# Row maxima of a 64 MB tensor: two load blocks in place of four, and eight late rows reduced by way of TensorE and GpSimd

## The chip, the cores and the metric

The kernel runs on one core of a Trainium2 chip. The metric is the device time in microseconds (us) of one execution; ten executions of the kernel before are shown below. Besides these times there is one profiled execution, whose span runs from the first to the last instruction that the hardware profiler recorded. Engines are named as in the profile: PE is TensorE, DVE is VectorE, ACT is ScalarE, POOL is GpSimd and SP is SyncE, which here only issues the loads.

## The reference

```python
def setup_inputs():
    batch, seq, dim = 32, 512, 1024
    return {"x": np.random.randn(batch, seq, dim).astype(np.float32)}

def reference(x):
    return np.max(x, axis=-1).astype(np.float32)
```

There are 32 x 512 = 16384 rows of 1024 floats (67.11 MB in), and the result is one maximum for each row (16384 floats out). A maximum costs one comparison for each element that is read.

## The kernel before

The 16384 rows are spread over the 128 partitions, so each partition has 128 rows of 4 KB. "A row" below always means one row on each of the 128 partitions, which is 512 KB. The rows are cut into four blocks of 42, 35, 34 and 17 rows per partition; inside a block a partition owns consecutive rows of `x`, so that a load of `g` rows reads `4 * g` KB in one piece for each partition. `BLOCKS` lists the loads of each block:

```python
BLOCKS = [
    [15, 14, 13],
    [11, 9, 8, 7],
    [6, 6, 5, 4, 4, 4, 3, 2],
    [2, 2, 2, 2, 2, 1, 1, 1, 1, 1, 1, 1],
]
RING = 46
```

One loop goes over the blocks and one inside it over the loads, 27 in all. For each load, SP issues a DMA of `g` rows into the next free place of `ring` (line 51), a buffer of 46 rows per partition in SBUF; when a load doesn't fit behind the last one, the place starts at 0 again (`at = 0`). VectorE then reduces these rows along the free dimension to `g` columns of `res` (line 52). `res` holds the 128 results of each partition. Behind each block ScalarE's queue issues a store of that block's columns (line 56). TensorE is not used, and GpSimd only fills four constants at the start.

The order is set by the tile framework. It keeps each engine's instructions in a list, puts a wait before a reduce for its load, and puts a wait before a load for the reduces that still read the place it overwrites. The loads also share eight completion semaphores in turn, so that a load waits for the landing of the load eight places ahead of it. SP issues in program order, and VectorE works in program order: a reduce that waits holds up all reduces behind it.

The wrapper at the end of the file only declares the tensors and launches the program. In the profile, a line 73 or 84 stands for the launch's own work at the start and at the end.

Of the kernel before, what the change touches and what calls it, by code (L numbers as in the profile page):

```python
# [1 line left out]

# [4 lines left out]


F32 = mybir.dt.float32

BLOCKS = [
    [15, 14, 13],
    [11, 9, 8, 7],
    [6, 6, 5, 4, 4, 4, 3, 2],
    [2, 2, 2, 2, 2, 1, 1, 1, 1, 1, 1, 1],
]
RING = 46


@with_exitstack
def kernel(
    ctx: ExitStack,
    tc: tile.TileContext,
    x: bass.AP,
    out: bass.AP,
):
    nc = tc.nc
    P = 128  # L30
    X = mybir.AxisListType.X

    xf = x.flatten_outer_dims()
    N, D = xf.shape
    I = N // P
    of = out.flatten_outer_dims()

    once = ctx.enter_context(tc.tile_pool(name="once", bufs=1))
    ring = once.tile([P, RING, D], F32)
    res = once.tile([P, I], F32)  # L40

    at = first = 0
    for loads in BLOCKS:
        S = sum(loads)
        xb = xf[first * P:(first + S) * P, :].rearrange("(p i) d -> p i d", p=P)
        b = 0
        for g in loads:
            if at + g > RING:
                at = 0
            xc = ring[:, at:at + g, :]  # L50
            nc.sync.dma_start(out=xc, in_=xb[:, b:b + g, :])  # L51
            nc.vector.reduce_max(out=res[:, first + b:first + b + g], in_=xc, axis=X)  # L52
            at += g
            b += g
        dst = bass.AP(tensor=of.tensor, offset=of.offset + first * P, ap=[[S, P], [1, S]])
        nc.scalar.dma_start(out=dst, in_=res[:, first:first + S])
        first += S
    assert first == I


# [1 line left out]
_INS = ['x']  # L62
_OUTS = [((32, 512), 'float32')]


# [23 lines left out]
```

## Time and profile before

| | us |
|---|---|
| median of 10 runs | 165.67 (165.49 to 165.97) |
| the profiled execution's own time | 165.66 |
| its span | 163.9 |
| VectorE busy, 27 reduces | 138.4 |
| VectorE's first reduce starts | 21.7 |
| VectorE's last reduce ends | 161.5 |
| GpSimd busy | 0.2 |
| bytes read, mean rate over the span | 67.11 MB, 410 GB/s |

The time of the profiled execution is 1.76 us longer than its span, and its last store takes 1.4 us to land. In the lines that follow, a group of instructions reads: line, engine, operation, output `<-` input, their shapes, and a count; then the busy time in us and the mean of one in ns; then the idle time of the engine just ahead of them and what ended it. A line of a load reads: tile `<-` tensor, queue, operation and count, the size in KB, and the us from its issue to its landing. SPq and ACTq are the queues of SP and ACT, and DVEq is VectorE's sequencer.

### The profile page before, as it was taken

Reading aid. Unit: us, or ns where it says so; the run is one execution under the profiler, and the core shown is the slowest. Engines: PE = TensorE matmul, PEld = TensorE weight load, DVE = VectorE, ACT = ScalarE, POOL = GpSimd, SP = SyncE. Lnnn points to the kernel's source line nnn. Section 1 sums busy time; section 2 is a strip of 40 time slices with the busy share of each in tenths; the row PEclk is TensorE's granted clock in tenths of the full one; section 3 lists DMA queues with packets and bytes.
Section 4 is the critical chain, followed back from the end, with each engine's and each line's share of the span. In section 5 each row is a group of like instructions: output and inputs, shape, how many; then the busy total and the mean of one; then the engine's idle time right before and its main releaser. Section 6 shows DMA issues by size and latency. Waiting matters only on the chain.

```text
span 163.9 us, 114 instructions
## 1 busy us (share of the span) xinstructions
DVE 138.4 (84%) x27; POOL 0.2 (0%) x4
## 2 busy tenths in 40 slices
DVE  0000079998999899999999999999999999999994
POOL 0000000000000000000000000000000000000000
DMA  7999699999999989999999999999999999999970
GB/s 240 480 480 450 270 448 448 448 448 416 416 416 449 495 352 528 414 433 420 402 408 440 441 407 468 396 455 408 421 440 436 409 425 418 422 420 416 404 310 2
DMA packets 4464, 67.18 MB, mean 410 GB/s; under 512 B 1008, under 2 KB 1008, under 8 KB 1904
## 3 DMA queue, kind: packets, MB, share of 16 engines
q1 hardware_dynamic: 3888, 67.11, 96.1%
q10 hardware_dynamic: 576, 0.07, 0.3%
HBM read 67.11 MB, written 0.07 MB: 410 GB/s over the span
## 4 chain that ended last, share of the span: by engine, by line
DVE 74%; DMA 23%; DVEq 1%; another core or an unknown queue 0%; SPq 0%; issue 0%
DVE res L52 74%; DMA ring<-in_x_dram 23%; DVEq L84 1%; SPq L51 0%
## 5 line engine op out<-in xcount | busy, mean ns | idle before, releaser
L52 DVE TENSOR_REDUCE res<-ring 128x1 f32<-128x1024 f32 (+12 forms) x27 | 138.4, 5200 | 23.1 <-DMA ring<-in_x_dram 23.1
L73 POOL MEMSET const-bfloat16-1.0<- 128x1 bf16 x1 | 0.1, 101 | 0.0
L73 POOL MEMSET const-uint8-127<- 128x1 uint8 x1 | 0.1, 101 | 0.0
L73 POOL MEMSET const-float32-0.0<- 128x1 f32 x1 | 0.1, 98 | 0.2 <-issue 0.2
L73 POOL MEMSET const-float32-1.0<- 128x1 f32 x1 | 0.1, 98 | 0.0
## 6 DMA issues: line engine op xcount, KB each, us to landing
ring<-in_x_dram SPq DMA_DIRECT2D x1, 7680.0 KB, 20.9
ring<-in_x_dram SPq DMA_DIRECT2D x1, 7168.0 KB, 37.4
ring<-in_x_dram SPq DMA_DIRECT2D x1, 6656.0 KB, 52.7
ring<-in_x_dram SPq DMA_DIRECT2D x2, 3072.0 KB, 33.4
ring<-in_x_dram SPq DMA_DIRECT2D x3, 2048.0 KB, 33.9
ring<-in_x_dram SPq DMA_DIRECT2D x6, 1024.0 KB, 24.0
ring<-in_x_dram SPq DMA_DIRECT2D x1, 5632.0 KB, 29.8
ring<-in_x_dram SPq DMA_DIRECT2D x1, 4608.0 KB, 24.9
```

What stands on the lines that cost most here:

```text
L52: nc.vector.reduce_max(out=res[:, first + b:first + b + g], in_=xc, axis=X)
L73: nc = _bacc.Bacc("TRN2", target_bir_lowering=False, num_devices=1)
L84: with _tile.TileContext(nc) as tc:
```

## The change

There are now two blocks, of 112 and 16 rows per partition, and the ring has 45 places. Each load is a triple `(n, m, w)`: `n` rows are loaded, the last `m` of them take a second route, and `w` is the number of the load behind whose reduce the result of that route is due. The loads are 15, 14, 14, 15, 15, 13, 12, 8 and 6 rows, then 4, 2, 2 and seven single rows, and the last row comes as two halves of 512 columns, one into `ring` and one into `tail`: 21 loads.

Eight rows take the second route (three of the seventh load, one of the eighth, two of the ninth, one of the tenth and one of the twelfth). For each of them TensorE turns the row's 1024 columns in eight transposes of 128 x 128 into PSUM (`ps`), so that the 128 partitions' rows lie along the free dimension; ScalarE copies `ps` to SBUF (`sb`); GpSimd takes the maximum over the partitions with `partition_all_reduce` (`top`); and eight small transposes turn `top` back into eight columns of `back`, one for each piece of 128 columns. VectorE then reduces these eight columns to the result. `backs` and `due` place the turns back and these last reduces in the program.

The identity matrix for the transposes is made on GpSimd behind the first load. The maximum of the last row's first half is written next to the second half in `tail`, and the last reduce takes both. Both stores now stand at the end of the program; the first of them is made to wait for the reduce of the last single row.

```diff
 BLOCKS = [
-    [15, 14, 13],
-    [11, 9, 8, 7],
-    [6, 6, 5, 4, 4, 4, 3, 2],
-    [2, 2, 2, 2, 2, 1, 1, 1, 1, 1, 1, 1],
+    [(15, 0, -1), (14, 0, -1), (14, 0, -1), (15, 0, -1), (15, 0, -1), (13, 0, -1), (12, 3, 7), (8, 1, 9), (6, 2, 12)],
+    [(4, 1, 14), (2, 0, -1), (2, 1, 17), (1, 0, -1), (1, 0, -1), (1, 0, -1), (1, 0, -1), (1, 0, -1), (1, 0, -1), (1, 0, -1)],
 ]
-RING = 46
+RING = 45
...
+    turn = ctx.enter_context(tc.tile_pool(name="turn", bufs=2))
+    allr = ctx.enter_context(tc.tile_pool(name="allr", bufs=2))
+    psum = ctx.enter_context(tc.tile_pool(name="psum", bufs=3, space=bass.MemoryType.PSUM))
+    psmall = ctx.enter_context(tc.tile_pool(name="psmall", bufs=2, space=bass.MemoryType.PSUM))
...
+    ident = once.tile([P, P], F32)
+    PAD = 16
+    tail = once.tile([P, PAD + H], F32)
+    backs = []
+    due = {}
+    def by_gpsimd(rows, cols, m):
+        back = psmall.tile([P, m, C], F32)
+        for k in range(m):
+            ps = psum.tile([P, D], F32)
+            for c in range(C):
+                nc.tensor.transpose(
+                    out=ps[:, c * P:(c + 1) * P],
+                    in_=rows[:, k, c * P:(c + 1) * P],
+                    identity=ident,
+                )
+            sb = turn.tile([P, D], F32)
+            nc.scalar.copy(out=sb, in_=ps)
+            top = allr.tile([P, D], F32)
+            nc.gpsimd.partition_all_reduce(top, sb, P, bass_isa.ReduceOp.max)
+            run(backs)
+            def turn_back(top=top, k=k):
+                for c in range(C):
+                    nc.tensor.transpose(
+                        out=back[:, k, c:c + 1],
+                        in_=top[0:1, c * P:(c + 1) * P],
+                        identity=ident[0:1, 0:1],
+                    )
+            backs.append(turn_back)
+        return lambda: nc.vector.reduce_max(out=cols, in_=back, axis=X)
+    def run(calls):
+        while calls:
+            calls.pop(0)()
...
-        for g in loads:
-            if at + g > RING:
+        for n, m, w in loads:
+            if at + n > RING:
                 at = 0
-            xc = ring[:, at:at + g, :]
-            nc.sync.dma_start(out=xc, in_=xb[:, b:b + g, :])
-            nc.vector.reduce_max(out=res[:, first + b:first + b + g], in_=xc, axis=X)
...
-        nc.scalar.dma_start(out=dst, in_=res[:, first:first + S])
+            xc = ring[:, at:at + n, :]
+            nc.sync.dma_start(out=xc, in_=xb[:, b:b + n, :])
+            cols = res[:, first + b:first + b + n]
+            if m:
+                due.setdefault(w, []).append(by_gpsimd(xc[:, n - m:, :], cols[:, n - m:], m))
+            else:
+                run(backs)
+            if j == 0:
+                nc.gpsimd.tensor_copy(out=ident[:, 0:1], in_=xc[:, 0, 0:1])
+                make_identity(nc, ident)
+            if n > m:
+                reduce = nc.vector.reduce_max(out=cols[:, :n - m], in_=xc[:, :n - m, :], axis=X)
+            run(due.get(j, []))
...
+    half = ring[:, at, :H]
+    nc.sync.dma_start(out=half, in_=xb[:, b, :H])
+    nc.sync.dma_start(out=tail[:, PAD:], in_=xb[:, b, H:])
+    nc.vector.reduce_max(out=tail[:, PAD - 1:PAD], in_=half, axis=X)
+    nc.vector.reduce_max(out=res[:, I - 1:], in_=tail[:, PAD - 1:], axis=X)
+    store = nc.scalar.dma_start(out=views[0][0], in_=views[0][1])
+    tc.add_manual_dep(store.ins, reduce.ins.name, SYNC, reason="behind the loads")
+    nc.scalar.dma_start(out=views[1][0], in_=views[1][1])
```

Here `D` is 1024, `P` 128, `C = D // P` is 8 and `H = D // 2` is 512.

More of the change, by code (lines that the diff above doesn't have):

```diff
@@ L6 @@
 from concourse._compat import with_exitstack
+from concourse import bass_isa
+from concourse.masks import make_identity
 F32 = mybir.dt.float32
 BLOCKS = [
-    [15, 14, 13],
-    [11, 9, 8, 7],
-    [6, 6, 5, 4, 4, 4, 3, 2],
-    [2, 2, 2, 2, 2, 1, 1, 1, 1, 1, 1, 1],
-]
-RING = 46
+    [(15, 0, -1), (14, 0, -1), (14, 0, -1), (15, 0, -1), (15, 0, -1), (13, 0, -1), (12, 3, 7), (8, 1, 9), (6, 2, 12)],
+    [(4, 1, 14), (2, 0, -1), (2, 1, 17), (1, 0, -1), (1, 0, -1), (1, 0, -1), (1, 0, -1), (1, 0, -1), (1, 0, -1), (1, 0, -1)],
+]
+RING = 45
+SYNC = mybir.DependencyInfo(mybir.DependencyClass.Sync, mybir.DependencyReason.DATA)
 @with_exitstack
@@ L34 @@
     N, D = xf.shape
+    H = D // 2
+    C = D // P
     I = N // P
@@ L38 @@
     once = ctx.enter_context(tc.tile_pool(name="once", bufs=1))
+    turn = ctx.enter_context(tc.tile_pool(name="turn", bufs=2))
+    allr = ctx.enter_context(tc.tile_pool(name="allr", bufs=2))
+    psum = ctx.enter_context(tc.tile_pool(name="psum", bufs=3, space=bass.MemoryType.PSUM))
+    psmall = ctx.enter_context(tc.tile_pool(name="psmall", bufs=2, space=bass.MemoryType.PSUM))
     ring = once.tile([P, RING, D], F32)
     res = once.tile([P, I], F32)
-    at = first = 0
+    ident = once.tile([P, P], F32)
@@ L43 @@
+    def run(calls):
+        while calls:
+            calls.pop(0)()
+    at = first = j = 0
+    views = []
     for loads in BLOCKS:
-        S = sum(loads)
+        S = sum(n for n, m, w in loads) + (loads is BLOCKS[-1])
         xb = xf[first * P:(first + S) * P, :].rearrange("(p i) d -> p i d", p=P)
+        dst = bass.AP(tensor=of.tensor, offset=of.offset + first * P, ap=[[S, P], [1, S]])
+        views.append((dst, res[:, first:first + S]))
         b = 0
-        for g in loads:
-            if at + g > RING:
+        for n, m, w in loads:
+            if at + n > RING:
@@ L49 @@
                 at = 0
-            xc = ring[:, at:at + g, :]
-            nc.sync.dma_start(out=xc, in_=xb[:, b:b + g, :])
[L52 to L55, printed above, removed]
-        nc.scalar.dma_start(out=dst, in_=res[:, first:first + S])
+            xc = ring[:, at:at + n, :]
+            nc.sync.dma_start(out=xc, in_=xb[:, b:b + n, :])
@@ L57 @@
+            at += n
+            b += n
+            j += 1
         first += S
     assert first == I
+    half = ring[:, at, :H]
[5 more added lines that the diff above has]
+    tc.add_manual_dep(store.ins, reduce.ins.name, SYNC, reason="behind the loads")
```

## The prediction

> **What bounds the kernel now.** I read the page's busy row and slices first, then the chain that ended last, then the reduces kept apart by shape, then the loads' times to landing.
>
> ```profile
> DVE 138.4 (84%) x27; POOL 0.2 (0%) x4
> ...
> DMA  7999699999999989999999999999999999999970
> ```
>
> Two resources look full: VectorE (DVE) and the DMA engines. The chain says which one ends last:
>
> ```profile
> 1.14 37.44 DMA ring<-in_x_dram
> 38.59 0.02 issue
> 38.61 15.09 DVE res L52
> 53.70 0.62 another core or an unknown queue
> 54.32 0.02 issue
> 54.34 106.06 DVE res L52 x24
> 160.40 1.13 DVEq L84
> ```
>
> Columns are start, length and what. After 54.34 us VectorE runs without a gap until 161.53, so VectorE ends the kernel. The shapes give its price per row:
>
> ```profile
> L52 DVE TENSOR_REDUCE res<-ring 128x15 f32<-128x15360 f32 x1 | 16.2, 16152 | 21.7 <-DMA ring<-in_x_dram 21.7
> L52 DVE TENSOR_REDUCE res<-ring 128x14 f32<-128x14336 f32 x1 | 15.1, 15087 | 0.8 <-DMA ring<-in_x_dram 0.8
> ...
> L52 DVE TENSOR_REDUCE res<-ring 128x1 f32<-128x1024 f32 x7 | 8.0, 1208 | 0.0
> ```
>
> One row more costs 16152 - 15087 = 1065 ns. A single row lasts 1208 ns, but the last two start at 159.2 and 160.3, about 1.13 us apart, so queued reduces overlap a little: I count 1.067 us a row plus 0.06 an instruction. Then the loads:
>
> ```profile
> ring<-in_x_dram SPq DMA_DIRECT2D x1, 7680.0 KB, 20.9
> ring<-in_x_dram SPq DMA_DIRECT2D x1, 7168.0 KB, 37.4
> ring<-in_x_dram SPq DMA_DIRECT2D x1, 6656.0 KB, 52.7
> ```
>
> Issued near 0.7, 1.1 and 1.6 us, they land at 21.6, 38.6 and 54.3: 32.7 us for 27 rows, 1.21 us a row, slower than VectorE's 1.07. The last load (issued at 150.2, landing 9.6 us later) lands at 159.8, and late single rows come 1.2 to 1.3 us apart. The loads therefore end 1.7 us before VectorE: that is nearly all there is to win, as every byte must still come.
>
> **What the Trainium skill says.** "DMA: Bandwidth & Descriptors", Where 436 GB/s comes from, puts the ports' ceiling at 435 GB/s, which is 1.205 us for a 512 KB row; 1.21 in this trace agrees, so the new load sizes cannot speed the stream. "VectorE: DVE Perf Modes", The perf-mode tier table, gives `tensor_reduce` one element a cycle only; 1065 ns for 1024 elements agrees. "GPSIMD Engine Reference", Performance versus the Vector engine, and Cross-partition, price the new operation below; nothing here shows it.
>
> **The change part by part.** *Loads.* Row counts landed become 15, 29, 43, 58, 73, 86, 98, 106, 112, 116 and on. At 1.21 us a row with some 0.05 us for each load the first seven land at 21.6, 38.6, 55.5, 73.7, 91.8, 107.6 and 122.2. VectorE waits for the second to fifth 0.9, 1.9, 3.1 and 2.0 us, and 0.2 for the seventh: 8 us in place of 1.4, so 6.6 lost. The seventh's nine rows end at 122.2 + 9.7 = 131.9. Ring space: the fifth load needs slots freed by the third reduce, at 70.6, while the fourth is in flight until 73.7; 3 us cover its start. Later loads wait only on reduces done by 122 and on earlier loads, so a late VectorE does not stop the stream. It ends at 159.3.
>
> *Reduces.* Left after 131.9: 7, 4, 3 and 2 rows (7.53 + 4.33 + 3.26 + 2.19), eight single rows (9.02), two half rows (0.59 + 0.68), five reduces of `back`, 8 to 24 elements (I take 0.15 each from a single row's 0.14 over its elements: 0.75). That is 28.35 us: without a further wait VectorE ends at 160.25, 1.3 us sooner. The half rows cost one instruction and spare waiting for the last half; the loads' end plus one half reduce, 160.0, bounds this from below.
>
> *The new route.* Each of eight rows takes eight TensorE transposes, a ScalarE copy, a GpSimd maximum and eight small transposes; then VectorE reads `back`. The diff interleaves them, but the changed program's TensorE list, as the scheduler leaves it (T a row's turn, B its turn back), is
>
> ```
> T1 T2 T3 B1 B2 B3 | T4 B4 | T5 T6 B5 B6 | T7 B7 | T8 B8
> ```
>
> and VectorE's list has the reduce of B1 to B3 *before* the eighth load's seven rows. Every bar makes GpSimd run dry: T4 stands behind B3, which waits for GpSimd's third maximum. Each group then pays turn, copy and turn back in series.
>
> Prices: "TensorE: Matmul & The Clock Gate", PE-mode transpose, gives 275 ns for a transpose in a kernel, for bf16; eight make 2.2 us. "ScalarE: Activation LUTs", What ACT_TABLE_LOAD costs, gives 186 ns + 0.833 ns an element: 1.0 us. Eight turns back of one column I take at 1.0 (half), hops between engines at 0.2: together c = 4.4 us, from 2.5 (if consecutive transposes take 0.1 us) to 6. The maximum X over 128 partitions by 1024 columns: I count some 14 operations a column (read, write, four folds of shuffle and maximum over a core's 16 lanes, four for the neighbours); at the page's three a cycle and 1.2 GHz that is 4.0 us. The page's own best loop takes 1.8 cycles where its ports allow 1.03, and that factor gives 7.0. I take X = 5.5. Ends: 1.5 us, the price of one plain loop over 1024 columns (1.8 cycles each); and 124 us, half the page's 247.7 us for a partition-axis reduce of 2048 columns.
>
> The chain starts at 122.2:
> - B3 done at 122.2 + 4.4 + 3 x 5.5 = 143.1; VectorE, free at 131.9, stands 11.2 us.
> - B4: 143.1 + 4.4 + 5.5 = 153.0; VectorE through its seven rows at 150.8: 2.2.
> - B6: 153.0 + 4.4 + 11.0 = 168.4; its four rows done at 157.5: 10.9.
> - B7: 178.3; 3 + 2 rows done at 174.0: 4.3.
> - B8: 188.2; three singles done at 181.8: 6.4.
>
> The stalls sum to 35.0 us; VectorE ends at 160.3 + 35.0 = 195.3. Behind each waiting reduce stand all later reduces, and both stores wait for the last of them.
>
> *Hidden parts.* The identity and GpSimd's library load start after the first landing at 21.6, 100 us before use. ScalarE's table load comes before its first copy. The first store (57 KB) now starts one single and two half reduces before the end; it should land beside the last one. If not, up to 1 us more.
>
> *Sum.* The profiled execution took 165.66 us: 161.53 to VectorE's end, 2.37 to the span's end (a store of 1.4 us and closing), 1.76 around the span; the median of the runs, 165.67, is the same. 195.3 + 2.4 + 1.7 = **199.4 us**. In general: 122.2 + 5c + 8X + 7.1 + 4.1.
>
> **The rivals.** *GpSimd is quick and the waits vanish.* VectorE ends at 160.3 and the time is 164.4. B8 must be done by 154.4, so X at most 1.3 us with c = 4.4, or 2.5 with c = 2.5. For it: VectorE does lose 8.5 us of rows. Against: the price of one plain loop would have to fold 128 partitions. 6%, and 2% for an end within 0.2% of before.
>
> *GpSimd reduces as slowly as the page's reduce:* X = 124 gives 122.2 + 22 + 992 + 11.2 = 1147 us. Nothing in the trace excludes it; the page's figure is for another instruction. Anything over X = 9.5: 7%.
>
> *The change doesn't do what it says in the other sense:* were the diff's interleaving kept, GpSimd would run without gaps from 125.4, and the end would be 125.4 + 8 x 5.5 + 1.1 + 7.1 + 4.1 = 181.7. The lists speak against it; 5%.
>
> *The stream slows* because rows of one partition now lie 448 KB and 64 KB apart instead of 68 to 168. Each per cent until the seventh landing adds 1.2 us. The chain stays the end, so it only widens the range.
>
> **How the numbers follow.** The main case, X from 3 to 9.5 us with the lists as they are, has 80%. Its ends: X = 3, c = 3 gives 172.5; X = 9, c = 5 gives 230.4. The range 172 to 230 takes in the interleaved case and leaves out the quick and the very slow one. Chances: faster by over 0.2% (about what a measurement of this kernel can tell from no change) 0.06, within 0.2% 0.02, slower 0.92.
>
> **What would show it.** Right: waits of VectorE for TensorE in five places, near 11, 2, 11, 4 and 6 us; five bursts of TensorE; GpSimd's maxima some 5.5 us apart inside a burst with a gap near 4 us between bursts; the last load landing near 159; VectorE free at 131.9. The prediction is wrong in its price if consecutive maxima start under 2 or over 9.5 us apart, in its order if T4 precedes B3 in the trace, and altogether if VectorE shows no wait for TensorE and ends near 160.

## The result, and the profile after

| | before | changed |
|---|---|---|
| median, us | 165.57 (165.40 to 165.97, 29 runs) | 181.9 (181.02 to 182.39, 8 runs) |
| ratio | 1 | 1.0972 [1.0958, 1.0987] |
| profiled execution: time, span | 165.66, 163.9 | 182.32, 180.5 |
| VectorE's last reduce ends | 161.5 | 178.1 |
| the last load lands | 159.9 | 161.3 |

The change makes the kernel 16.3 us slower. The forecast was slower by 33.7: the direction and the mechanism held, and one price was far too high. The lines below, of the changed kernel, are the page's busy time of each engine and the share of the DMA engines in 40 slices of the span (9 is 90% or more); the prediction shows the same lines of before:

```profile
PE 21.6 (12%) x128; PEld 19.4 (11%) x128; DVE 130.7 (72%) x26; ACT 9.4 (5%) x9; POOL 26.6 (15%) x15
...
DMA  6999999999999999999989989999999999920000
```

VectorE has 7.7 us less to do (130.7 in place of 138.4), and still ends 16.6 us later. The DMA row is full through its 35th slice and then empty: in the last 19 us there is nothing left to load, and no engine is busy all the time. So something waits. The list of waits (engine, line, what it waited for: total us, times, longest) says what:

```profile
POOL top L74 <- ACT sb L72: 110.9, 5, 94.3
DVE res L115 <- DMA ring<-in_x_dram: 31.7, 6, 21.4
...
DVE res L86 <- PE back L79: 15.7, 4, 5.9
```

VectorE waits 15.7 us for TensorE's turns back, in four places; before, nothing of the kind existed. It also waits 31.7 us for loads, where it waited 23.1 before. That accounts for its later end: 15.7 + 8.6 - 7.7 = 16.6. GpSimd waited 94.3 us for its first row, and four times more for ScalarE's copies, together 16.6 us. The timeline of one pass from bar to bar shows how the two belong together. Its columns are start, length, engine, line and operation, and in brackets the idle time just ahead and what ended it:

```profile
127.50 9.68 POOL L74 PARTITION_ALL_REDUCE top<-sb  x3 [94.28 <-ACT sb L72]
...
137.23 1.01 PE L79 MATMUL back<-ident,top 1*128 1x1 f32 x8 [2.19 <-POOL top L74]
138.17 1.57 PEld L66 LDWEIGHTS ps<-ident,ring 128*128 128x128 f32 x8
138.18 1.97 PE L66 MATMUL ps<-ident,ring 128*128 128x128 f32 x8
138.28 0.18 DVE L86 TENSOR_REDUCE res<-back 128x3 f32<-128x24 f32 x1 [4.26 <-PE back L79]
138.38 7.61 DVE L115 TENSOR_REDUCE res<-ring 128x7 f32<-128x7168 f32 x1
140.24 1.01 ACT L72 COPY sb<-ps 128x1024 f32<-128x1024 f32 x1 [8.45 <-PE ps L66]
141.34 3.22 POOL L74 PARTITION_ALL_REDUCE top<-sb  x1 [4.16 <-ACT sb L72]
```

Three maxima end at 137.2. Only then does TensorE turn the third one back (1.01 us) and, behind that, turn the fourth row (1.97), which had been in SBUF since about 134; ScalarE copies it (1.01), and GpSimd, dry for 4.16 us, starts again. VectorE stood 4.26 us for the turn back, with seven loaded rows queued behind. The same bracket, 4.16, stands at each of the four bars (a bar is a place in TensorE's order where the turn of a row stands behind a turn back that waits for GpSimd).

### The profile page after: what moved, and what is told of

Read it like the earlier page. It is cut to its first block, busy times and chain, and to the rows that moved or that the text cites. A ratio compares the mean times of both kernels' runs of the same rounds, so it can differ in the third digit from the quotient of the medians.

```text
span 180.5 us, 400 instructions
## 1 busy us (share of the span) xinstructions
PE 21.6 (12%) x128; PEld 19.4 (11%) x128; DVE 130.7 (72%) x26; ACT 9.4 (5%) x9; POOL 26.6 (15%) x15
## 4 chain that ended last, share of the span: by engine, by line
DMA 50%; DVE 22%; POOL 11%; PE 7%; issue 4%; ACT 2%; POOLq 2%; ACTq 0%; SPq 0%
DMA ring<-in_x_dram 50%; DVE res L115 21%; POOL top L74 11%; PE ps L66 4%; ACT sb L72 2%; PE back L79 2%; POOLq L158 2%; DVE res L127 0%; DVE tail L126 0%; ACTq L72 0%; DVE res L86 0%; SPq L104 0%
## 5 line engine op out<-in xcount | busy, mean ns | idle before, releaser
L115 DVE TENSOR_REDUCE res<-ring 128x1 f32<-128x1024 f32 (+8 forms) x19 | 129.0, 6826 | 31.7 <-DMA ring<-in_x_dram 31.7
L74 POOL PARTITION_ALL_REDUCE top<-sb x8 | 25.8, 3256 | 110.9 <-ACT sb L72 110.9
L66 PE MATMUL ps<-ident,ring 128*128 128x128 f32 x64 | 14.5, 416 | 124.4 <-DMA ring<-in_x_dram 124.4
L66 PEld LDWEIGHTS ps<-ident,ring 128*128 128x128 f32 x64 | 12.7, 223 | 124.4 <-issue 124.3
L72 ACT COPY sb<-ps 128x1024 f32<-128x1024 f32 x8 | 8.1, 1013 | 156.5 <-PE ps L66 154.8
L86 DVE TENSOR_REDUCE res<-back 128x1 f32<-128x8 f32 (+2 forms) x5 | 0.8, 169 | 15.7 <-PE back L79 15.7
L79 PE MATMUL back<-ident,top 1*128 1x1 f32 x64 | 7.4, 232 | 25.0 <-POOL top L74 25.0
L79 PEld LDWEIGHTS back<-ident,top 1*128 1x128 f32 x64 | 6.7, 194 | 27.1 <-POOL top L74 27.1
masks.py:199 POOL TENSOR_SCALAR_AFFINE_SELECT ident<-ident 128x128 f32<-128x128 f32 x1 | 0.3, 282 | 11.1 <-issue 11.1
L127 DVE TENSOR_REDUCE res<-tail 128x1 f32<-128x513 f32 x1 | 0.7, 686 | 0.0
L126 DVE TENSOR_REDUCE tail<-ring 128x1 f32<-128x512 f32 x1 | 0.7, 676 | 0.0
```

The source lines that it names most:

```text
L66: nc.tensor.transpose(out=ps[:, c * P:(c + 1) * P], in_=rows[:, k, c * P:(c + 1) * P], identity=ident,)
L72: nc.scalar.copy(out=sb, in_=ps)
L74: nc.gpsimd.partition_all_reduce(top, sb, P, bass_isa.ReduceOp.max)
L79: nc.tensor.transpose(out=back[:, k, c:c + 1], in_=top[0:1, c * P:(c + 1) * P], identity=ident[0:1, 0:1],)
L86: return lambda: nc.vector.reduce_max(out=cols, in_=back, axis=X)
L115: reduce = nc.vector.reduce_max(out=cols[:, :n - m], in_=xc[:, :n - m, :], axis=X)
```

## The experiments

Ratios are against runs of the kernel before on the same chip; differences between two experiments are between medians, some of them from different chips. In the code, `...` stands for parts that are not shown. A load has 16 completions, one for each DMA engine, and "spread" below is the time from the first of them to the last, read from the trace.

**The loads alone.** All `m` are 0, and the identity is left out.

```diff
-    [..., (12, 3, 7), (8, 1, 9), (6, 2, 12)],
-    [(4, 1, 14), (2, 0, -1), (2, 1, 17), (1, 0, -1), ...],
+    [..., (12, 0, -1), (8, 0, -1), (6, 0, -1)],
+    [(4, 0, -1), (2, 0, -1), (2, 0, -1), (1, 0, -1), ...],
-            if j == 0:
-                nc.gpsimd.tensor_copy(out=ident[:, 0:1], in_=xc[:, 0, 0:1])
-                make_identity(nc, ident)
```

> The change's loads, halves and late stores alone; all 128 rows are reduced by VectorE and TensorE, ScalarE and GpSimd do nothing. Theory (the waits in TensorE's order are the loss, and the larger early loads cost on their own because VectorE stands 8 us for them instead of 1.4): VectorE ends near 167.8 to 168.5 and the time is about 172, slower than before by 6 us, and the late starts of the third and fifth loads stay if they come from the ring. Rival (the loads are harmless, all of the loss is the new route): within 1 us of before, 165 to 166. Rival (the loads are most of the loss): 178 or more.

Measured: 172.92 us, 1.0426 [1.0404, 1.0448]. From the timeline of VectorE:

```profile
122.37 44.60 DVE L111 TENSOR_REDUCE res<-ring 128x12 f32<-128x12288 f32 x13 [0.16 <-DMA ring<-in_x_dram]
166.90 0.68 DVE L122 TENSOR_REDUCE tail<-ring 128x1 f32<-128x512 f32 x1
167.61 0.69 DVE L123 TENSOR_REDUCE res<-tail 128x1 f32<-128x513 f32 x1
```

From 122.4 on VectorE never waits and ends at 168.3, with the last load landed since 159.5. The new loads alone cost 7.2 us: VectorE stands for the large early ones and can't make it up. The route has to earn that first.

**The order of the source.** TensorE's and VectorE's instructions are held in the order in which they are written, by an edge from each to the one before it on its engine that makes nothing wait.

```diff
+    keep = tc.keep_in_program_order
-                nc.tensor.transpose(...)
+                keep(nc.tensor.transpose(...))
-        return lambda: nc.vector.reduce_max(out=cols, in_=back, axis=X)
+        return lambda: keep(nc.vector.reduce_max(out=cols, in_=back, axis=X))
```

> The changed kernel with TensorE's and VectorE's instructions held in the order of the source: each turn back stands behind the next row's turn, each reduce of turned maxima at its due place. Theory (the order is the loss): GpSimd runs its maxima about 3.2 us apart as far as the loads allow, VectorE's waits for TensorE vanish, VectorE ends about 162.5 and the time is 166 to 167, within 1 us of before. Rival (the route's own price is the loss: eight maxima and what surrounds them are too long whatever the order): above 175. Rival (GpSimd slows VectorE or the loads by sharing memory): VectorE's reduces of one row last longer than 1.21 us and the time stays above 170.

Measured: 169.87 us, 1.0246 [1.0231, 1.0262]: 12 us of the loss are gone, but 3 more than the theory left stay. Near the end of the timeline one bar is still there:

```profile
158.93 3.22 POOL L75 PARTITION_ALL_REDUCE top<-sb  x1 [4.16 <-ACT sb L73]
...
163.25 0.17 DVE L87 TENSOR_REDUCE res<-back 128x1 f32<-128x8 f32 x1 [3.55 <-PE back L80]
```

The source itself makes this bar: at the eleventh load, which has no row for the route, `run(backs)` issues the seventh row's turn back ahead of the eighth row's turn. I had not followed that branch.

**No bars.** That one call is left out until the twelfth load is past.

```diff
-            else:
+            elif j > 11:
                 run(backs)
```

> The order of the source once more, but the seventh row's turn back is no longer issued at the eleventh load: it stands behind the eighth row's turn, so that no turn of a row waits for a maximum. In the run before this one that last bar left VectorE 3.5 us of waiting. Theory (each bar in TensorE's order is a wait of VectorE): no wait of VectorE for TensorE over 0.3 us; VectorE ends with the loads, near 162.6, and the time is 166.2 to 166.6, some 0.4% slower than before, since the last load lands near 161.1 instead of 159.9. Rival (GpSimd cannot keep up late: three rows come in the last 12 us): a wait of 2 us or more stays ahead of a late reduce of turned maxima and the time stays above 168.

Measured: 166.22 us, 1.0048 [1.0029, 1.0068]. VectorE's waits for TensorE are gone from the list; its last reduce ends at 162.1, 1.3 us behind the last landing at 160.8. The time lies in the 166.2 to 166.6 that was expected. The timeline of the first rows has this in place of the bar shown above:

```profile
126.94 6.47 POOL L75 PARTITION_ALL_REDUCE top<-sb  x2 [93.15 <-ACT sb L73]
...
134.35 6.45 POOL L75 PARTITION_ALL_REDUCE top<-sb  x2 [0.93 <-ACT sb L73]
```

The instructions are the same as in the changed kernel; only their order differs. The order therefore costs 181.9 - 166.2 = 15.7 us, the figure in the list of waits. TensorE's clock is not the cause: the mean that the chip granted was 0.88 of full speed in the profiled execution of the changed kernel and 1.0 in this one, and a row's turn took up to 1.97 us and a turn back up to 1.01 in both.

**Each maximum twice**, with the changed kernel's own order pinned on both engines. For that order the call of `run(backs)` and the due places `w` were moved too, which the lines do not show.

```diff
+            mid = allr.tile([P, D], F32)
-            nc.gpsimd.partition_all_reduce(top, sb, P, bass_isa.ReduceOp.max)
+            nc.gpsimd.partition_all_reduce(mid, sb, P, bass_isa.ReduceOp.max)
+            nc.gpsimd.partition_all_reduce(top, mid, P, bass_isa.ReduceOp.max)
```

> The changed kernel, in its own order on TensorE and VectorE, with GpSimd's maximum taken twice in a row for each of the eight rows. Theory (one chain through five bursts sets the end, and each maximum lies on it with its full 3.22 us): the time grows by 8 x 3.22 = 25.8 us to 207.7. Rival (part of the maxima lies beside VectorE's reduces and costs nothing): growth well under 20 us. Rival (GpSimd's fixed costs at the start of each are much of it): growth near 25.8 as well, so this run does not tell that apart.

Measured: 208.18 us (two runs), 26.3 above the changed kernel. Its list of waits has

```profile
DVE res L88 <- PE back L80: 41.9, 5, 14.0
```

26.2 more than 15.7, for eight maxima more of 3.2 us each. What was added to the maxima reaches the end in full: all eight lie on the chain.

**The route alone.** The loads, ring and stores of before, with eight late rows on the route, in the scheduler's order.

```diff
-    [6, 6, 5, 4, 4, 4, 3, 2],
-    [2, 2, 2, 2, 2, 1, 1, 1, 1, 1, 1, 1],
+    [(6, 0, -1), (6, 0, -1), (5, 0, -1), (4, 0, -1), (4, 3, 12), (4, 1, 14), (3, 0, -1), (2, 2, 17)],
+    [(2, 0, -1), (2, 0, -1), (2, 1, 19), (2, 0, -1), (2, 1, 22), (1, 0, -1), ...],
```

> The kernel before with its 27 loads, its ring and its four stores, but eight late rows take the new route, in the order that the scheduler leaves. TensorE's order here has four groups in place of five. Theory (chain of groups): from the landing of the first three rows near 123, four times 4.2 us and eight times 3.2 us and what is left behind the last turn back, 6 us: VectorE ends near 170 to 172, the time is 174 to 176. Rival (early loads carry the loss): near before, under 168. Rival (the loss of loads and route add up to the 16.3 us): 165.6 + 16.3 - 6.4 = 175.5, which the theory shares; the waits in the trace tell these apart.

Measured: 182.14 us, 1.0980 [1.0961, 1.0999], against 174 to 176 expected. I had put the first three rows one load too early: they land at 129.0, not 123, as the timeline shows.

```profile
129.07 4.50 PE L68 MATMUL ps<-ident,ring 128*128 128x128 f32 x24 [129.07 <-DMA ring<-in_x_dram]
...
172.30 0.17 DVE L88 TENSOR_REDUCE res<-back 128x1 f32<-128x8 f32 x1 [3.84 <-PE back L81]
```

From there to the last reduce of turned maxima the chain takes 43.2 us; four groups of 4.2 and eight maxima of 3.22 make 42.6. The mechanism holds without the new loads. VectorE's delay also reached the stream here: the ring is reused to the end, the last two loads were issued only at 159.2 and 159.6 and landed at 163.1 and 164.3.

**What delays the loads.** In the run without bars the last load lands 0.9 us later than before, although there are fewer loads. Two kernels with the loads alone and unused maxima on GpSimd (three of 1024 columns, two each of 512, 256 and 128) tell what GpSimd does to the stream; they differ in when it starts. In the late one these instructions are held behind the identity, in the early one nothing holds them back.

```diff
+                src = turn.tile([P, D], F32)
+                nc.gpsimd.memset(src, 1.0)
+                for width in (1024, 1024, 1024, 512, 512, 256, 256, 128, 128):
+                    top = allr.tile([P, D], F32)
+                    nc.gpsimd.partition_all_reduce(top[:, :width], src[:, :width], P, bass_isa.ReduceOp.max)
```

> The loads alone (as in the run of the loads alone), and on GpSimd behind the first load the identity and then nine maxima over partitions of a constant tile: three of 1024 columns, two each of 512, 256 and 128; no other engine uses them. Theory (GpSimd's start of its library, near 22 to 33 us, holds up one DMA engine): the 16 completions of a load spread over 0.5 us for the first load and over 1.2 us or more from the second on, about 2 us from the fifth, and the last load lands near 161 instead of 159.5. Rival (TensorE's, ScalarE's or GpSimd's late work slows the stream): it lands near 159.5. Price: 3.2 us for 1024 columns; if the cost is all by column, 0.4 us for 128, if half is fixed, 1.8 us.

Measured: the spread is 0.5 us at the first load, 0.6 at the second, 1.7 at the third and 1.3 from the fifth on; the last load lands at 160.2, between the two expectations. GpSimd stands idle twice:

```profile
33.16 0.28 POOL masks.py:199 TENSOR_SCALAR_AFFINE_SELECT ident<-ident 128x128 f32<-128x128 f32 x1 [11.36 <-issue]
33.41 0.94 POOL L115 MEMSET src<- 128x1024 f32 x1
44.87 16.67 POOL L118 PARTITION_ALL_REDUCE top<-src  x9 [10.52 <-issue]
```

I took these stretches for the start of GpSimd's library, and call the runs so; the trace does not name them, and shows only that they are gone when a maximum stands at the start (next run). In each of them, at 27 and 40 us, a few packets of the loads last 0.6 to 1.2 us longer than their neighbours. In all six traces in which GpSimd stands idle like this (the changed kernel among them) the spread grows by the third load, by 0.8 to 1.4 us; in the other eight it does not. The maxima start 3.20 us apart for 1024 columns, 1.77 for 512, 1.05 for 256 and 0.69 for 128: 2.8 ns a column and 0.33 us fixed.

> As the run with the library started late, but GpSimd's constant tile, its library and the nine maxima come at the start, beside the first load. Theory (the start of the library holds up a DMA engine whenever it comes): the first load's spread grows from 0.5 to 1 us or more and stays, and the last load lands near 160.5 to 161. Rival (only a start in the midst of the stream disturbs it): spread 0.5 us, the last load lands near 159.5.

Measured: with the library at the start there is no idle stretch, the spread stays at 0.6 us through the fourth load, then jumps to 1.9 at the fifth, and the last load lands at 160.2 as well. The theory as I wrote it falls: an early start costs the first four loads nothing, and what remains begins at the fifth. Nor does the last landing tell the late start from the early one, since the step at the fifth load differs from trace to trace.

**The ring.** The loads alone with the first seven changed so that the fifth lies exactly in the place of the second.

```diff
-    [(15, 0, -1), (14, 0, -1), (14, 0, -1), (15, 0, -1), (15, 0, -1), (13, 0, -1), (12, 0, -1), ...],
+    [(15, 0, -1), (15, 0, -1), (14, 0, -1), (15, 0, -1), (15, 0, -1), (13, 0, -1), (11, 0, -1), ...],
```

> The loads alone again, but the first seven are 15, 15, 14, 15, 15, 13, 11: the fifth load then lies exactly where the second was and needs only its reduce, so it is issued near 56 us instead of 71. In the run of the loads alone the spread of the 16 completions went from 0.5 to 1.0 us at the fifth load and its packets near 72 us took longer. Theory (a load issued under 2 us before the stream reaches it starts slowly): the spread stays near 0.5 us and the last load lands at 158.9 to 159.1 instead of 159.5; the time changes by under 0.5 us from 172.9, since VectorE ends last. Rival (the slow packets belong to the place in memory or the size): the spread grows at the fifth load as before.

Measured: the spread stays at 0.5 us from the first load to the last, which lands at 159.0 instead of 159.5; 171.71 us (one run), 1.2 below the median of the loads alone and 0.7 below their profiled execution, where I had expected under 0.5. With the loads alone the fifth was issued at 70.4 us and its first packet started at 72.4; here it was issued at 55.7, with the same size and place in the ring. In all eight traces in which it is issued at 70 to 72 us some of its packets last 0.7 to 1.3 us longer than the usual 2.27; in the three in which it is issued at 56 none does. So a load issued only some 2 us before the DMA engines come to it starts slowly.

**Library first**, in the kernel without bars, and then **the swapped loads** as well.

```diff
+    warm = once.tile([P, 32], F32)
+    nc.gpsimd.memset(warm[:, :16], 1.0)
+    nc.gpsimd.partition_all_reduce(warm[:, 16:], warm[:, :16], P, bass_isa.ReduceOp.max)
+    make_identity(nc, ident)
```

> The run without bars, but GpSimd makes the identity and takes a first small maximum at the very start, so that its library comes before the loads; the hold behind the first load is gone. Theory (two starts of the library near 22 to 44 us hold up a DMA engine; before the stream they cost nothing): the spread of completions is 0.5 to 0.6 us until the fifth load and 1.0 to 1.9 after it, the last load lands near 160 instead of 160.8, the time is 165.3 to 166.0. Rival (the maxima themselves disturb the stream): as without, 166.2.

> As the run with the library first, with the loads 15, 15, 14, 15, 15, 13, 11 at the start. Theory (order, library and ring are all that stood between the change and its gain): the last load lands near 159.1, VectorE ends 1.3 us later near 160.4, the time is 164.3 to 164.8, faster than before by 0.5 to 0.8%. Rival (VectorE's late reduces of turned maxima or GpSimd's lateness take the place of it): VectorE ends over 2 us after the last landing and the time stays at 165.5 or more.

Measured: 165.86 us, 1.0019 [1.0008, 1.0030], with the library first, inside the expected 165.3 to 166.0, though its interval just touches that of the run without bars; 165.71 us, 1.0000 [0.9990, 1.0011], with both. The last one misses its 164.3 to 164.8. The spread stays at 0.6 us until 149, as meant, and then goes to 1.9 with the load that lands at 151.3, and the last load lands at 160.3. The DMA queues in the stretch from 147 to 153 us (packets, MB, share of 16 engines):

```profile
q1 hardware_dynamic: 620, 2.40, 99.5%
q8 instruction: 1, 0.02, 1.1%
```

One transfer of 16 KB of instructions, 1.1% of 16 engines over 6 us, is some 1.1 us of a single engine, at a time when the loads keep the engines 99.5% busy.

**Four rows on the route**, with the library first and the swapped loads.

```diff
-    [..., (11, 3, 7), (8, 1, 9), (6, 2, 12)],
-    [(4, 1, 14), (2, 0, -1), (2, 1, 17), (1, 0, -1), ...],
+    [..., (11, 3, 7), (8, 1, 11), (6, 0, -1)],
+    [(4, 0, -1), (2, 0, -1), (2, 0, -1), (1, 0, -1), ...],
```

> As the run with the library first and the swapped loads, but only the first four of the eight rows take the new route, so TensorE has 64 matmuls in place of 128; VectorE reduces the other four. In the run before, the completions' spread went from 0.6 to 1.9 us near 149.5, just where a transfer of 16 KB of instructions took 1.09 us on one DMA engine. Theory (that fetch of TensorE's later instructions is what holds up one engine there): no such transfer, the spread stays near 0.6 us to the end, and the last load lands near 159.0 in place of 160.3; VectorE, with four rows more, ends near 164.5 and the time is 168 to 169. Rival (the maxima or transposes slow the stream near the end): the spread grows after 125 us although there is no fetch.

Measured (one run): no such transfer, spread 0.5 us to the end, the last load at 158.9; 167.78 us, since VectorE has four rows more and ends at 163.7. With half of TensorE's instructions both the fetch and the step in the spread are gone. Four maxima between 125 and 140 us left the spread as it was. The completions of single engines say more. In three traces the fetch comes with several loads still to follow: at 149.0 us in the run with both, at 149.5 with the library first, at 155.6 in the changed kernel. In each of them, from the next load on, one completion of the 16 stands about 1.5 us later than it did and the other 15 where they were. In the changed kernel that engine had been early (it goes from 0.2 to 1.7 us behind the first), so the spread of 2.3 us did not show it. That the fetch is the cause is the likely reading: no run moved the fetch alone. In the run without bars (159.9) and the route alone (156.4) it came when the engines had two rows or less left to load, and made no step.

**Finer loads without the route.** The kernel before with 28 sizes worked out from its own rates, the last row in two halves.

```diff
-    [15, 14, 13],
-    [11, 9, 8, 7],
-    [6, 6, 5, 4, 4, 4, 3, 2],
-    [2, 2, 2, 2, 2, 1, 1, 1, 1, 1, 1, 1],
+    [14, 14, 12],
+    [11, 9, 7, 7],
+    [7, 5, 5, 5, 3, 4, 3, 3, 3],
+    [2, 2, 2, 2, 1, 1, 1, 1, 1, 1, 1, 1],
```

> The kernel before with loads of 14, 14, 12, 11, 9, 7, 7, 7, 5, 5, 5, 3, 4, 3, 3, 3, then 2, 2, 2, 2 and seven single rows, and the last row in two halves; nothing on the other engines. Worked out with the rates of before (1.209 us a row plus 0.02 to 0.07 a load, 1.067 us a row plus 0.06 a reduce). Theory (VectorE ends last because it starts late, and only its lag of 1.7 us behind the loads can be won): VectorE ends near 160.8, the time is 164.8 to 165.2, faster than before by 0.3 to 0.5%. Rival (the number of loads or their size sets the rate of the stream): the last load lands later than 160.3 and nothing is won.

Measured: 165.22 us, 0.9977 [0.9967, 0.9986], the only version faster than before, by 0.2%; that is just outside the 164.8 to 165.2 and the 0.3 to 0.5% that were expected. The timeline of VectorE ends with

```profile
159.69 0.68 DVE L57 TENSOR_REDUCE tail<-ring 128x1 f32<-128x512 f32 x1
160.40 0.69 DVE L58 TENSOR_REDUCE res<-tail 128x1 f32<-128x513 f32 x1
```

and the last load lands at 159.8. VectorE's lag behind the loads has gone from 1.7 us to 1.3. This small gain needed no second engine.

## Why the prediction was right and where it was wrong

**The mechanism was right.** TensorE's order, the place of the reduces of `back` on VectorE, the five groups, the first store hidden beside the last reduces: all stand in the trace. The loads' cost of 6.6 us was 7.2 in the run of the loads alone; in the changed kernel VectorE's waits for loads grew by 8.6. Set against the sum:

| term | predicted, us | measured, us | effect |
|---|---|---|---|
| seventh load lands | 122.2 | 124.2 | + 2.0 |
| 5 c | 5 x 4.4 = 22.0 | 3.3 + 4 x 4.16 + 1.1 = 21.0 | - 1.0 |
| 8 X | 8 x 5.5 = 44.0 | 25.8 | - 18.2 |
| behind the last turn back | 7.1 | 7.1 | 0 |
| VectorE's end to the full time | 4.1 | 4.2 | + 0.1 |
| sum | 199.4 | 182.3 | - 17.1 |

**The step that failed is X**, the price of GpSimd's maximum. The groups of the changed kernel give it beside the other two prices:

```profile
L74 POOL PARTITION_ALL_REDUCE top<-sb x8 | 25.8, 3256 | 110.9 <-ACT sb L72 110.9
L66 PE MATMUL ps<-ident,ring 128*128 128x128 f32 x64 | 14.5, 416 | 124.4 <-DMA ring<-in_x_dram 124.4
L72 ACT COPY sb<-ps 128x1024 f32<-128x1024 f32 x8 | 8.1, 1013 | 156.5 <-PE ps L66 154.8
```

A maximum lasts 3.26 us, and consecutive ones start 3.2 apart where 5.5 was taken: 2.8 ns a column, which I estimate as 3.4 cycles at the 1.2 GHz that the Trainium skill gives in "GPSIMD Engine Reference", Specifications. My count of 14 operations at three a cycle, 4.7 cycles, was already above that, and the loop factor on top of it pushed the choice to 5.5. Why the count is too long stays open, as no run shows how the instruction folds the partitions. The range of 1.5 to 124 us from the skill's prices held the value. Its upper end, half the figure in Cross-partition of the same page, is 38 times too high; as the prediction said, that figure is for another instruction. The skill's prices in "TensorE: Matmul & The Clock Gate", PE-mode transpose, and "ScalarE: Activation LUTs", What ACT_TABLE_LOAD costs, agree with the trace: a row's eight turns took 1.97 us (2.2 from the page), its copy 1.01 (1.0). The turns back took 1.01 (1.0, my own half).

Because X was smaller, VectorE's waits were 4.3, 0, 5.9, 1.8 and 3.8 us where 11.2, 2.2, 10.9, 4.3 and 6.4 were forecast: 15.7 in place of 35.0. The second vanished, since the fourth row was back just when the seven rows were done.

**Two things put down as free were not.** "3 us cover its start", of the fifth load: it was issued at 71 and did start slowly, as the swapped loads show. And the library start "100 us before use": GpSimd's 11 us of standing cost it nothing, but the spread of the loads grew there. A load has landed when the last of its 16 completions is in, so the delays of different DMA engines don't add up, and the 2.0 us of the seventh landing are not split between the two here. The last load, forecast for 159.3, landed at 161.3; VectorE was by then behind the loads, so this cost nothing more.

**The rivals.** The interleaved case was put at 181.7, close to what came, but by chance: it supposed that GpSimd runs without gaps, and the trace has the gap at every bar. Held in the order of the source the kernel takes 169.9, and without that order's last bar 166.2. The quick case did not come about, for its X of 1.3 us is less than half of 3.2. (Its limit has a slip: for an end at 160.3 the eighth row must be back by 153.2, not 154.4, so X at most 1.1.) The slow case, X of 124, is excluded by the same 3.2. The rows' distance of 448 KB slowed nothing: with the loads alone the first four landed where 1.21 us a row puts them.

**Where the gain went.** The loads alone cost 7.2 us against before; the route without bars brings back 6.7 (172.9 to 166.2); the order takes 15.7. With all that was found taken out, but for the fetch of instructions, the kernel only comes level, since before VectorE ended only 1.7 us behind the last load.

## What to carry to other kernels

Read the order of instructions that was built, not that of the source, whenever work passes through an in-order engine twice: one short instruction that waits for a slow engine, ahead of the next item's start, turns a pipeline into a chain. Before moving work off an engine, look how far it ends behind the work that cannot be made less, here the loads; that was 1.7 us, and moving eight rows could not win more while every byte still had to come. When a price is not in the trace, keep its whole range: here a choice inside it that rested on counted operations was off by 1.7 times.

## What was not expected of the hardware

- When the affine select and the first maximum came in the midst of the load stream, GpSimd stood idle, 11.1 us ahead of the affine select in the changed kernel (11.4 and 10.5 us, two stretches, in the run with the late library), and a few load packets lasted up to 1.2 us longer; with a maximum at the start of the program neither was seen.
- The maximum over 128 partitions costs 0.33 us and 2.8 ns a column.
- Here a DMA engine that fell behind in the full stream stayed behind: a spread of completions, once grown, mostly stayed to the last load. A 16 KB instruction transfer of 1.1 us came with one engine's completions 1.5 us later from there on, in three traces.
